# Inverse square roots moved from ten small VectorE steps to one GpSimd power operation

## The chip, the core and the metric

The kernel runs on one core of one Trainium2 chip. The metric is the device time of one execution in microseconds (us); three runs of the kernel before gave 2031.2, 2032.12 and 2036.46 us, median 2032.12 us. The engines are named as the profile names them: PE is TensorE (PEld its weight loads), DVE is VectorE, ACT is ScalarE, POOL is GpSimd, SP is SyncE, which here only issues DMAs.

## What is computed

One inference step of a two-layer decoder trunk of width 1024, for 1024 prompt tokens and 64 sample tokens with shared weights. Layer 0 is a gated short convolution beside a 4-head memory cross-attention, layer 1 is a multi-head latent attention of 8 heads beside another memory cross-attention; each has one input projection, a SiLU gate, one output projection and a residual. What matters here is how often an inverse root of a mean square occurs:

```python
def rms_norm(x, g):
    xf = x.astype(jnp.float32)
    y = xf * lax.rsqrt(jnp.mean(xf * xf, axis=-1, keepdims=True) + EPS)
    return (y * g.astype(jnp.float32)).astype(x.dtype)
```

It is taken of the tokens at the entry of both layers, of the memory and of its keys, of every memory query head (`mem_q_g`), of both latents of layer 1 (`q_lora_g`, `ckv_g`), of every query head, and, as `kscale = rsqrt(ms + EPS)`, of every key head of the latent attention.

## The kernel before

Activations lie feature-major, 128 features on the partitions and tokens along the free dimension, so a sum of squares over features is a matmul with ones. It gives a small tile of one value per token: 128 partitions by 1 to 16 columns. On this tile the inverse root is taken. A full-precision product is made of three matmuls (`mm3`, L189 to L191) on a value split into a high part (written by ACT, L183) and a low part, which is a subtraction of two SBUF tiles (`sub`, L179) on DVE or on POOL: the low parts of weights (`wli`, `wlo`, `wlv`) are mostly POOL's.

The prompt runs in two groups: A (256 prompt tokens and the 64 sample tokens) and B (768 prompt tokens). Two generators are interleaved: one does the memory keys and values, group B, the prompt attention of layer 1 (`mla`) and the last output product; the other does group A and the sample tokens, whose paged attention gathers its cache rows by indirect DMAs that POOL issues (`nat`, L1078). Within each engine the order of the instructions is then set by the scheduler of the tile framework, from its own estimates of durations; on the chip every engine works through its list in that order. So a change of one operation can move its neighbours.

The helper that the change rewrites and its callers, with the line numbers of the profile:

```python
196  def rsqrt_(p, out, v, shape):
202      V.tensor_scalar(out=out.bitcast(I32), in0=v.bitcast(I32), scalar1=-0.5, scalar2=float(0x5F3759DF), ...)
203      for _ in range(3):
204          V.tensor_tensor(out=t, in0=out, in1=out, op=ALU.mult)
205          V.scalar_tensor_tensor(out=t, in0=t, scalar=-0.5, in1=v, op0=ALU.mult, op1=ALU.mult)
206          V.scalar_tensor_tensor(out=out, in0=t, scalar=1.5, in1=out, op0=ALU.add, op1=ALU.mult)
...
478                  rsqrt_(pp, rs, v, [128, nt])
479                  V.tensor_scalar(out=rs, in0=rs, scalar1=MSC, scalar2=None, op0=ALU.mult)
...
1368         rsqrt_(p, rs, v, [128, 16])
1371         T.transpose(tk[0:8, 0:128], rs[:, 0:8], ident)
1379         V.scalar_tensor_tensor(out=rq, in0=rs[:, 8:16], scalar=SM, in1=rcq[:, 0:8], ...)
```

It is called 48 times: 16 times in `mem_part` (L478; tiles `mv_`, `mrs`; four heads, two layers, two groups), 9 times for the kv latent of layer 1 (L857; `cs1` to `cr1`, printed `cs` and `cr`, then `ckn` L859), 8 times in `prep` of the prompt attention (L1368; `akv` to `aks`, once per head, prepared while the head before is attended), and 15 times elsewhere (entry norms `strxa`, `strxb`, `strcq`, `strn`, memory `strm`, `ksr`, sample tokens `smr`, `ks_`, `rq`).

In the prompt attention each block of 128 queries is: scores on PE (L1410 to L1416), scaling by the key factor and running maximum on DVE (`ass`, L1418), the exponential on ACT (L1423), transposes of the weights on PE (`atp`, L1442) into one of two PSUM tiles, their split by ACT (`aPTH`) and DVE (`aPTL`, L179), and the value product on PE (`aO`).

Of the kernel before, what the change touches and what calls it, by code (L numbers as in the profile page):

```python
# [5 lines left out]
F = mybir.dt.float32  # L6
R = mybir.dt.float32r
I32 = mybir.dt.int32
# [16 lines left out]
EPS = 1e-6  # L25
# [59 lines left out]
# packed small vectors, one column each of [128, NV]  # L85
VG0, VG1, VGM, VGQL, VGQ, VGK, VMQ, VCW = 0, 8, 16, 32, 35, 36, 37, 39
NV = VCW + 24
# packed rows that are broadcast over partitions
# [4 lines left out]
def build(nc, tc, I, O):  # L93
# [50 lines left out]
    G.memset(ones, 1.0)  # L144
    rows = pc.tile([128, RMK], F, name="rows")
# [47 lines left out]
    cnt = [0]  # L193
    sm = {}

    def rsqrt_(p, out, v, shape):
        """out = v ** -0.5 by Newton steps from an integer seed."""
        cnt[0] += 1
        t = p.tile(shape, F, tag="rsq", name=f"rsq{cnt[0]}")
        P = shape[0]  # L200
        t, out, v = t[0:P], out, v
        V.tensor_scalar(out=out.bitcast(I32), in0=v.bitcast(I32), scalar1=-0.5, scalar2=float(0x5F3759DF), op0=ALU.mult, op1=ALU.add)
        for _ in range(3):
            V.tensor_tensor(out=t, in0=out, in1=out, op=ALU.mult)
            V.scalar_tensor_tensor(out=t, in0=t, scalar=-0.5, in1=v, op0=ALU.mult, op1=ALU.mult)
            V.scalar_tensor_tensor(out=out, in0=t, scalar=1.5, in1=out, op0=ALU.add, op1=ALU.mult)

    def stat_r(p, sqs, tiles, n, tag, eps=EPS, keep=None):
        """per token rsqrt(sum over features / n + EPS): [128, len(tiles)]; sqs: list of [128, T] squares."""
        nt = len(tiles)  # L210
        ps = pst("x", "stat" + tag)
        for i, (c0, m) in enumerate(tiles):
            for j, sq in enumerate(sqs):
                T.matmul(ps[0:m, 2 * i:2 * i + 2], sq[:, c0:c0 + m], ones[:, 0:2], start=(j == 0), stop=(j == len(sqs) - 1))
        v = (keep or p).tile([128, nt], F, name="stv" + tag, tag="stv" + (tag if keep else ""))
        r = (keep or p).tile([128, nt], F, name="str" + tag, tag="str" + (tag if keep else ""))
        if tiles[-1][1] < 128:
            V.memset(v, 1.0)
        for i0, i1, m in ([(0, nt, 128)] if tiles[-1][1] == 128 else [(0, nt - 1, 128), (nt - 1, nt, tiles[-1][1])]):
            V.tensor_scalar(out=v[0:m, i0:i1], in0=ps[0:m, 2 * i0:2 * i1].rearrange("p (i two) -> p i two", two=2)[:, :, 0], scalar1=1.0 / n, scalar2=eps, op0=ALU.mult, op1=ALU.add)  # L220
        rsqrt_(p, r, v, [128, nt])
        return v, r

    def bcast_tok(p, r, tiles, Tn, tag):
        """r [128 tokens, tile] -> list of (c0, n, psum [128, n]) with r along the free dim on all partitions."""
        out = []
        for b0 in range(0, len(tiles), 4):
            ts = tiles[b0:b0 + 4]
            ps = pst("s" if len(tiles) > 4 else "x", "bc" + tag)
            base_ = ts[0][0]  # L230
            for i, (c0, m) in enumerate(ts):
                d = p.tile([128, 128], F, name="dg" + tag, tag="dg", bufs=2)
                V.tensor_scalar(out=d[0:m, 0:m], in0=ident[0:m, 0:m], scalar1=r[0:m, b0 + i:b0 + i + 1], scalar2=None, op0=ALU.mult)
                T.matmul(ps[:, c0 - base_:c0 - base_ + m], ones[0:m, :], d[0:m, 0:m], start=True, stop=True)
            out.append((base_, ts[-1][0] + ts[-1][1] - base_, ps))
        return out
# [5 lines left out]
    def scale_T(xk, gcol, xH, xL):  # L242
        """split of x * g, not yet divided by the RMS"""
        for k in range(8):
            split_g(xH[:, k, :], xL[:, k, :], xk(k), gcol + k)

    def norm_T(pt, x, gcol, tiles, Tn, xH, xL, tag, le="g", ae=None, load=None):
        """x [128, 8, T] raw (feature-major) -> split of x * rsqrt(mean sq) * g."""
# [27 lines left out]
    class Stream:  # L276
        """weights: load two ahead, split one ahead."""
# [6 lines left out]
        def load_part(self, j, n):  # L284
            """one of n parts of the first unit"""
# [15 lines left out]
        def parts(self):  # L301
            """the splits of the next unit, as a list of calls"""
# [25 lines left out]
    def fm(ps, n, w, nk, xH, xL, c0):  # L328
        """feature-major product of one unit of 128 channels."""
# [96 lines left out]
    def mem_part(l, g, pp, ws, qi, xH, xL, ydst, done, pq, rb=None, fill=None):  # L426
        """memory attention of a group, head by head; ydst(h) holds the gate first and then the result"""
# [8 lines left out]
        def qpart(h, d):  # L436
            """q of head h: halves of q^T and the per token scale"""
# [100 lines left out]
    def samples(l, g, pp, nb):  # L538
        """memory attention of the sample tokens; the first step only starts loads"""
# [62 lines left out]
    def silu2(p, out, ps, n, rb=None):  # L602
        """out = 2 z sigmoid(z) = (tanh(z / 2) + 1) z, z = ps or ps * rb"""
# [7 lines left out]
    # persistent small tiles  # L611
# [109 lines left out]
    def out0(g, get, xsrc, acc, keep, px=None, held=None, wpre=()):  # L721
        """x1 = x + y W_out for the group; acc = sum of squares per feature row; held gets what remains to be done for the last unit"""
# [64 lines left out]
    def rope(p, out, src, cc, ss, m, nh, tag):  # L787
        """out, src [m, nh, 64]; cc, ss [m, 64]"""
# [9 lines left out]
    def in1_kv(g, ws, pp, xH, xL, rb):  # L798
        """latents: cq (feature-major), ckv and kpe (natural)"""
# [121 lines left out]
    def samp_prep():  # L921
# [23 lines left out]
        # k_nope of the own keys, only for their RMS factor  # L945
# [23 lines left out]
        # q  # L969
# [41 lines left out]
        # raw copies in (b, h, t) order  # L1011
# [13 lines left out]
        # scores against the own keys, all batches: [64 (h, t), b, 64 keys]  # L1025
# [25 lines left out]
    def samp_attn():  # L1051
        """keys 0..63 of a page on partitions 0..63 of the scores, keys 64..127 on the others, each with its own running maximum"""
# [4 lines left out]
        NU, UB, CU = 64, 8, 2  # units of 8 pages: all, in a batch row, in a softmax block  # L1057
# [157 lines left out]
    def mla_load(p):  # L1215
        """latents and tables that the preparation of the attention reads"""
        cq = p.tile([128, 3, NP], F, name="lcq")
        S.dma_start(out=cq, in_=d_cq)
        sm["pre"] = cq, rope_tab(p, 0, 8)
# [316 lines left out]
    def samp_y():  # L1536
        """sample attention output of layer 1: value up-projection and gate"""
# [28 lines left out]
    def out1_pre():  # L1566
        """first weights and gated branches of the output product, before the last head ends"""
# [68 lines left out]
    def group_a(g, xin):  # L1636
        """layer 0 for the first group of tokens; its result stays on chip, ready for layer 1"""
# [30 lines left out]
    def group_b(g, xin):  # L1668
        """layer 0 for the other tokens; gated branches and result wait in DRAM"""
# [63 lines left out]
    class Rows:  # L1733
        """separate tiles of features, read like one tile"""
# [45 lines left out]
    def interleave(a, b, rat):  # L1780
        """emit steps of a and b; in each part of b, a takes rat times the time of b; a waits at a name until b has passed it"""
# [157 lines left out]
```

## Time and profile before

| | before |
|---|---|
| time, median of three runs | 2032.12 us |
| span of the profiled execution, first to last instruction | 2030.3 us |
| mean granted TensorE clock over the span | 0.982 |
| PE busy | 1934.9 us, 95% |
| DVE busy | 979.2 us, 48% |
| ACT busy | 744.7 us, 37% |
| POOL busy | 669.5 us, 33% |
| DMA, mean | 181 GB/s |

The time of the profiled execution itself was not listed; its span is 1.8 us under the median and 0.9 us under the fastest run. An engine's share of busy time is an average over stages: PE is near full in most of them, and what is left of it idle lies in the first 50 us (32.0 us busy), between 150 and 200 us (37.5 us busy of 50), and in the prompt attention from 1570 to 1900 us (306.4 us busy of 330).

### The profile page before, as it was taken

What the parts mean: (1) busy time and instruction counts of PE and PEld (TensorE: products, weight loads), DVE (VectorE), ACT (ScalarE), POOL (GpSimd) and SP (SyncE); (2) the same over time, 40 slices, a digit from 0 to 9 for tenths busy, and PEclk for the clock granted to TensorE, in tenths of its full rate; (3) what the DMA queues carried; (4) which work ended last, traced back from release to release, by engine and by line L of the source; (5) the groups of instructions that cost most, each with busy time, mean ns of one, the idle gap of its engine ahead of it and who ended that gap; (6) DMA issues with size and microseconds to landing.
All of it is one profiled execution on the core that took longest, in us unless ns stands there. A gap on an engine that the chain in (4) does not pass through costs nothing. (4 is left out here: it accounts for less than half of the span.)

```text
span 2030.3 us, 33997 instructions
## 1 busy us (share of the span) xinstructions
PE 1934.9 (95%) x11740; PEld 1619.7 (80%) x11740; DVE 979.2 (48%) x2450; ACT 744.7 (37%) x1499; POOL 669.5 (33%) x589
## 2 busy tenths in 40 slices
PE   6997999999999999999999999999998899999999
PEld 5987998998997867667777765777687687787999
DVE  7659444456644533444323443344456656657300
ACT  6434323333321223333222322333333666667300
POOL 4544433422220223233434324333333334433220
PEclk8999999999999999999999999999999999999999
DMA  6552535442535487687988878877852311114532
GB/s 222 168 198 94 179 117 197 145 143 88 176 131 194 136 266 247 226 303 242 339 298 273 278 259 271 264 254 235 270 178 70 93 57 58 59 46 129 179 96 73
DMA packets 192877, 368.17 MB, mean 181 GB/s; under 512 B 27809, under 2 KB 135585, under 8 KB 191426
## 3 DMA queue, kind: packets, MB, share of 16 engines
q1 hardware_dynamic: 172178, 298.75, 44.7%
q0 software_dynamic: 20528, 67.26, 10.2%
q8 instruction: 93, 1.52, 0.3%
q14 instruction: 78, 0.64, 0.1%
HBM read 331.22 MB, written 34.70 MB: 180 GB/s over the span
## 5 line engine op out<-in xcount | busy, mean ns | idle before, releaser
L1078 POOL DMA_INDIRECT nat<-nat,IX x256 | 274.2, 1071 | 490.4 <-PE pv L1152 422.0
L189 PE MATMUL mm<-xH,whi 128*128 128x384 f32 (+1 forms) x1112 | 372.4, 335 | 9.7 <-ACT whi L183 5.1
L191 PE MATMUL mm<-xH,wli 128*128 128x384 f32 (+1 forms) x1112 | 367.1, 330 | 6.1 <-POOL wli L179 4.2
L190 PE MATMUL mm<-xL,whi 128*128 128x384 f32 (+1 forms) x1112 | 366.9, 330 | 0.8 <-DVE xL L179 0.8
L189 PEld LDWEIGHTS mm<-xH,whi 128*128 128x128 f32 x1112 | 213.8, 192 | 32.2 <-issue 13.3
L183 ACT ACTIVATE whi<-wri 128x1024 fp32r<-128x1024 f32 (+1 forms) x130 | 126.1, 977 | 271.1 <-PE mm L190 202.6
L191 PEld LDWEIGHTS mm<-xH,wli 128*128 128x128 f32 x1112 | 213.6, 192 | 8.3 <-POOL wli L179 5.3
L190 PEld LDWEIGHTS mm<-xL,whi 128*128 128x128 f32 x1112 | 213.8, 192 | 4.1 <-issue 2.4
L179 POOL TENSOR_TENSOR wli<-wri,whi 128x1024 fp32r<-128x1024 f32 (+1 forms) x65 | 146.9, 2264 | 161.2 <-ACT whi L183 161.0
L1087 PE MATMUL sAB<-rec,qar 128*64 128x512 f32 x512 | 153.5, 602 | 0.4 <-DMA rec<-rec 0.2
L1152 PE MATMUL pv<-nat,PT 128*64 128x256 f32 x1024 | 140.9, 392 | 4.8 <-ACT PT L1132 4.0
L1152 PEld LDWEIGHTS pv<-nat,PT 128*64 128x64 f32 x1024 | 75.6, 138 | 55.4 <-issue 13.5
L179 DVE TENSOR_TENSOR wli<-wri,whi 128x1024 fp32r<-128x1024 f32 (+1 forms) x65 | 72.8, 1124 | 72.1 <-ACT whi L183 69.9
L189 PE MATMUL mm<-nH,whi 128*128 128x384 f32 x304 | 105.6, 347 | 0.5 <-issue 0.5
L190 PE MATMUL mm<-nL,whi 128*128 128x384 f32 x304 | 102.4, 338 | 0.0
L191 PE MATMUL mm<-nH,wli 128*128 128x384 f32 x304 | 102.3, 337 | 0.0
L179 POOL TENSOR_TENSOR wlo<-wro,who 128x768 fp32r<-128x768 f32 (+3 forms) x30 | 59.2, 1978 | 118.0 <-ACT who L183 117.9
L189 PE MATMUL mm<-yHo,who 128*128 128x384 f32 (+1 forms) x288 | 97.1, 337 | 0.9 <-ACT yHo L183 0.9
L183 ACT ACTIVATE who<-wro 128x768 fp32r<-128x768 f32 (+3 forms) x44 | 38.1, 873 | 155.9 <-PE mm L190 117.7
L191 PE MATMUL mm<-yHo,wlo 128*128 128x384 f32 (+1 forms) x288 | 94.3, 327 | 0.0
L190 PE MATMUL mm<-yLo,who 128*128 128x384 f32 (+1 forms) x288 | 93.9, 326 | 0.0
L1089 PE MATMUL sAB<-rec,QPE 128*64 128x512 f32 x256 | 91.2, 596 | 0.0
(595 smaller groups left out, 4336.9 us busy)
## 6 DMA issues: line engine op xcount, KB each, us to landing
rec<-rec SPq DMA_DIRECT2D x512, 192.0 KB
wri<-wi SPq DMA_DIRECT2D x114, 512.0 KB
wro<-wo SPq DMA_DIRECT2D x29, 384.0 KB
smkv<-ckm SPq DMA_DIRECT2D x16, 512.0 KB
smkv<-cvm SPq DMA_DIRECT2D x16, 512.0 KB
wrm<-memw SPq DMA_DIRECT2D x7, 1024.0 KB
wro<-wo SPq DMA_DIRECT2D x7, 768.0 KB
yld<-d_ys SPq DMA_DIRECT2D x8, 544.0 KB
```

The lines of the kernel that those rows point to most:

```text
L179: eng.tensor_tensor(out=out, in0=a, in1=h.bitcast(F), op=ALU.subtract)
L183: A.activation(h, src, AF.Copy)
L189: T.matmul(out, wh, xh, start=first, stop=False)
L190: T.matmul(out, wh, xl, start=False, stop=False)
L191: T.matmul(out, wl, xh, start=False, stop=last)
L1078: G.indirect_dma_start(out=t[:, j % 2, :], out_offset=None, in_=I["nat"], in_offset=bass.IndirectOffsetOnAxis(ap=IX[:, q:q + 1], axis=0), ...
L1087: T.matmul(o, QA[:, cb, b, :], t[:, :, cb * 128 + ab * 64:cb * 128 + ab * 64 + 64], start=(cb == 0), stop=False)
L1089: T.matmul(o, QPE[:, b, ab, :], t[:, :, 256:320], start=False, stop=True)
L1152: T.matmul(d["v"][64 * ab:64 * ab + 64, 0:256], PT[:, j, ab, :], n[j][:, ab * 256:ab * 256 + 256], start=(i == 0 and j == 0), stop=(i == C ...
```

## The change

`rsqrt_` becomes one POOL instruction that raises the tile to the power -0.5, given as a constant tile `mhalf`, written once at the start. The scratch tile `rsq` goes away. Comments and docstrings are dropped too, so that line numbers after L144 are 2 higher, and after `rsqrt_` 7 lower.

```diff
     ones = pc.tile([128, 128], F, name="ones")
     G.memset(ones, 1.0)
+    mhalf = pc.tile([128, 16], F, name="mhalf")
+    G.memset(mhalf, -0.5)
...
     def rsqrt_(p, out, v, shape):
-        cnt[0] += 1
-        t = p.tile(shape, F, tag="rsq", name=f"rsq{cnt[0]}")
-        P = shape[0]
-        t, out, v = t[0:P], out, v
-        V.tensor_scalar(out=out.bitcast(I32), in0=v.bitcast(I32), scalar1=-0.5, scalar2=float(0x5F3759DF), op0=ALU.mult, op1=ALU.add)
-        for _ in range(3):
-            V.tensor_tensor(out=t, in0=out, in1=out, op=ALU.mult)
-            V.scalar_tensor_tensor(out=t, in0=t, scalar=-0.5, in1=v, op0=ALU.mult, op1=ALU.mult)
-            V.scalar_tensor_tensor(out=out, in0=t, scalar=1.5, in1=out, op0=ALU.add, op1=ALU.mult)
+
+        G.tensor_tensor(out=out, in0=v, in1=mhalf[0:shape[0], 0:shape[1]], op=ALU.pow)
```

The scheduler places the new instruction and what hangs on it anew. Three places show how. The first is DVE in the prompt attention, where the fourth head is prepared; before, the ten steps from `akv` to `aks`, of which the first seven are seen here, were mixed with the scaling of scores (`ass`) and the split of weights (`aPTL`):

```order
L1367 TENSOR_SCALAR akv<-akv 128x16
L202 TENSOR_SCALAR aks<-akv 128x16
L204 TENSOR_TENSOR rsq_21471<-aks 128x16
L205 SCALAR_TENSOR_TENSOR rsq_21471<-rsq_21471,akv 128x16
L206 SCALAR_TENSOR_TENSOR aks<-rsq_21471,aks 128x16
L204 TENSOR_TENSOR rsq_21471<-aks 128x16
L205 SCALAR_TENSOR_TENSOR rsq_21471<-rsq_21471,akv 128x16
L1418 ISA ass,amx<-mm,akb 128x512
L1418 ISA amx 128x1
L206 SCALAR_TENSOR_TENSOR aks<-rsq_21471,aks 128x16
L179 TENSOR_TENSOR aPTL<-atp,aPTH 128x4x128
```

The same stretch of DVE in the changed kernel:

```order
L1360 TENSOR_SCALAR akv<-akv 128x16
L1372 SCALAR_TENSOR_TENSOR arq<-aks,rcq 128x8
L1411 ISA ass,amx<-mm,akb 128x512
L1411 ISA amx 128x1
L181 TENSOR_TENSOR aPTL<-atp,aPTH 128x4x128
```

The reader of the result, `arq`, has moved up from behind all ten steps to the place directly behind their input, ahead of `ass` and `aPTL`. On POOL, in the same stretch, the splits of values (`avH`, `avL`) and of weights (`wlv`) stood alone before:

```order
L1310 CAST avH<-araw 128x512
L179 TENSOR_TENSOR avL<-araw,avH 128x512
L1310 CAST avH<-araw 128x512
L179 TENSOR_TENSOR avL<-araw,avH 128x512
L179 TENSOR_TENSOR wlv<-wrv,whv 128x512
```

and now have the power among them:

```order
L1303 CAST avH<-araw 128x512
L181 TENSOR_TENSOR avL<-araw,avH 128x512
L1303 CAST avH<-araw 128x512
L199 TENSOR_TENSOR aks<-akv,mhalf 128x16
L181 TENSOR_TENSOR avL<-araw,avH 128x512
L181 TENSOR_TENSOR wlv<-wrv,whv 128x512
```

It stands behind the second cast and ahead of that cast's subtraction. The second place is PE in that stretch, where `tk` is the transpose that reads the result:

```order
L1416 MATMUL mm<-cmb,idb 128x128
L1442 MATMUL atp<-ident,ass 128x128 x4
L189 MATMUL aO<-aPTH,avH 128x256
L1410 MATMUL mm<-akH,aqH 128x512
L1442 MATMUL atp<-ident,ass 128x128
L190 MATMUL aO<-aPTL,avH 128x256
```

In the changed kernel the rows at this point are:

```order
L1409 MATMUL mm<-cmb,idb 128x128
L1364 MATMUL tk<-ident,aks 8x128
L1435 MATMUL atp<-ident,ass 128x128 x5
L191 MATMUL aO<-aPTH,avH 128x256
L192 MATMUL aO<-aPTL,avH 128x256
```

`tk`, which stood six rows below the first piece, is now ahead of the transposes `atp`, and one value product and one score product that stood between the fourth and the fifth `atp` now come behind the fifth. The third place is DVE in the memory attention of layer 0, group A, third head, where `yr` is the gate and `xL` a low part for group B:

```order
L477 TENSOR_SCALAR mv__1978<-mst 128x2
L202 TENSOR_SCALAR mrs<-mv__1978 128x2
L204 TENSOR_TENSOR rsq_1981<-mrs 128x2
L205 SCALAR_TENSOR_TENSOR rsq_1981<-rsq_1981,mv__1978 128x2
L179 TENSOR_TENSOR xL<-xnxb,xH 128x768
L609 SCALAR_TENSOR_TENSOR yr_442<-slt,mm 128x320
```

In the changed kernel:

```order
L470 TENSOR_SCALAR mv__1910<-mst 128x2
L181 TENSOR_TENSOR xL<-xnxb,xH 128x768
L602 SCALAR_TENSOR_TENSOR yr_424<-slt,mm 128x320
L472 TENSOR_SCALAR mrs<-mrs 128x2
L265 SCALAR_TENSOR_TENSOR xnxb<-x,vec,bcxb 128x256
```

Three of the ten steps stood ahead of `xL` and `yr`; now nothing does, and the scaling of the result (L472) comes behind both.

## Rows read from the trace of the kernel before

**Rows 1.** The page: the span, the busy time of each engine with its share of the span and its instructions, and the TensorE clock that was granted, in tenths of full speed, in 40 equal slices of the span.

```profile
span 2030.3 us, 33997 instructions
PE 1934.9 (95%) x11740; PEld 1619.7 (80%) x11740; DVE 979.2 (48%) x2450; ACT 744.7 (37%) x1499; POOL 669.5 (33%) x589
...
PEclk8999999999999999999999999999999999999999
```

**Rows 2.** Busy time by window, of the instructions that read or write the scratch tile `rsq` alone (L204 to L206, nine of the ten steps of each call), over the whole span; then the clock and the DMA share of that stretch.

```profile
0.00:2030.30 2030.30, 98.32 (x432) 0.98 0.55 181
```

**Rows 3.** The waits of PE: who waited <- for whom: us in total, times, longest us.

```profile
PE atp L1442 <- DVE rsq L204: 7.0, 5, 2.4
...
PE mst L471 <- DVE msq L452: 4.1, 2, 3.7
PE mm L189 <- DVE yr L609: 4.1, 2, 3.6
...
PE ckt L873 <- DVE ckn L859: 3.3, 3, 2.4
```

**Rows 4.** The timeline in the prompt attention where the fourth head is prepared: start us, length us, engine, line, operation, out<-in, shape, count, and in brackets the idle time before it and what ended it. DVE first, then POOL, then PE.

```profile
1685.17 0.18 DVE L1367 TENSOR_SCALAR akv<-akv 128x16 f32<-128x16 f32 x1
...
1686.30 1.16 DVE L206 SCALAR_TENSOR_TENSOR aks<-rsq,aks 128x16 f32<-128x16 f32 x1
...
1689.51 0.68 DVE L179 TENSOR_TENSOR aPTL<-atp,aPTH 128x512 fp32r<-128x512 f32 x1
...
1685.41 0.62 POOL L1310 CAST avH<-araw 128x512 fp32r<-128x512 f32 x1 [2.77 <-ACT araw L1309]
1686.11 1.31 POOL L179 TENSOR_TENSOR avL<-araw,avH 128x512 fp32r<-128x512 f32 x1
1687.38 1.27 POOL L179 TENSOR_TENSOR wlv<-wrv,whv 128x512 fp32r<-128x512 f32 x1
...
1690.34 0.30 PE L1442 MATMUL atp<-ident,ass 128*128 128x128 f32 x1 [2.38 <-DVE rsq L204]
```

**Rows 5.** The same timeline where the third head is prepared and POOL has nothing to do; DVE, then PE.

```profile
1646.41 0.17 DVE L1367 TENSOR_SCALAR akv<-akv 128x16 f32<-128x16 f32 x1
...
1648.45 0.68 DVE L179 TENSOR_TENSOR aPTL<-atp,aPTH 128x512 fp32r<-128x512 f32 x1
...
1647.95 0.39 PE L189 MATMUL aO<-aPTH,avH 128*128 128x256 f32 x1 [0.24 <-ACT aPTH L183]
1648.18 0.40 PE L1410 MATMUL mm<-akH,aqH 128*128 128x512 f32 x1
1649.28 0.30 PE L1442 MATMUL atp<-ident,ass 128*128 128x128 f32 x1 [0.70 <-DVE rsq L204]
```

**Rows 6.** The same timeline where the first head is prepared: DVE's first step, and PE's transpose of the result.

```profile
1583.61 0.17 DVE L202 TENSOR_SCALAR aks<-akv 128x16 int32<-128x16 int32 x1
...
1589.09 0.27 PE L1371 MATMUL tk<-ident,aks 128*8 128x128 f32 x1 [2.60 <-DVE aks L206]
```

**Rows 7.** The timeline of layer 0, group A, memory attention, third head: DVE, POOL, PE.

```profile
176.23 1.74 DVE L204 TENSOR_TENSOR rsq<-mrs 128x2 f32<-128x2 f32 x1
178.00 2.27 DVE L205 SCALAR_TENSOR_TENSOR rsq<-rsq,mv__1978 128x2 f32<-128x2 f32 x1
...
181.06 0.47 DVE L609 SCALAR_TENSOR_TENSOR yr<-slt,mm 128x320 f32<-128x320 f32 x1
...
173.78 2.38 POOL L179 TENSOR_TENSOR wli<-wri,whi 128x1024 fp32r<-128x1024 f32 x1 [7.46 <-ACT whi L183]
176.13 1.82 POOL L179 TENSOR_TENSOR xL<-xnxb,xH 128x768 fp32r<-128x768 f32 x1
177.92 2.33 POOL L179 TENSOR_TENSOR wli<-wri,whi 128x1024 fp32r<-128x1024 f32 x1
...
181.59 0.64 PE L189 MATMUL mm<-xH,whi 128*128 128x320 f32 x1 [3.62 <-DVE yr L609]
```

**Rows 8.** Two windows by engine: start and end, length, then busy us (instructions) of PE, PEld, DVE, ACT and POOL, the granted clock, the DMA share and GB/s.

```profile
179.60:186.40 6.80, 4.81 (x19) 4.81 (x20) 6.34 (x18) 1.47 (x2) 1.08 (x2) 0.50 0.24 77
1589.30:1592.70 3.40, 3.40 (x13) 2.82 (x12) 0.50 (x3) 0.41 (x1) 0.00 (x0) 0.50 0.44 130
```

**Rows 9.** POOL's groups by line and shape: the two small operations with two input tiles; busy us, mean ns of one, then the idle time before.

```profile
L794 POOL TENSOR_TENSOR rp2k<-kg,rtab 128x64 f32<-128x64 f32 x8 | 2.6, 328 | 39.2 <-DVE kg L862 33.1 <-DMA rec<-rec 5.9
...
L161 POOL TENSOR_TENSOR gq<-vec 128x1 f32<-128x1 f32 x1 | 0.2, 190 | 1.4 <-DMA vec<-vec 1.4
```

**Rows 10.** The timeline near the start, at the entry norm of group A: POOL, then PE.

```profile
24.47 4.66 POOL L179 TENSOR_TENSOR wlm<-wrm,whm 128x1024 fp32r<-128x1024 f32 x2 [3.65 <-ACT whm L183]
...
31.18 1.81 PE L234 MATMUL bcxa<-dgxa,ones 128*128 128x128 f32 x6 [5.97 <-DVE dgxa L233]
```

**Rows 11.** The timeline at one of the nine calls for the kv latent, while POOL issues gathers: DVE's first step and the reader of the result, then POOL.

```profile
1251.44 0.15 DVE L202 TENSOR_SCALAR cr<-cs 128x1 int32<-128x1 int32 x1
...
1253.56 0.48 DVE L859 SCALAR_TENSOR_TENSOR ckn<-mm,cr,rows 128x256 f32<-128x256 f32 x1 [0.21 <-DVE cr L206]
...
1251.37 1.01 POOL L1078 DMA_INDIRECT nat<-nat,IX  x1 [0.30 <-issue]
```

**Rows 12.** The timeline of DVE in the memory attention of layer 1, group A, first head: the first of the ten steps, and the reader of the result.

```profile
476.70 2.23 DVE L202 TENSOR_SCALAR mrs<-mv__4885 128x2 int32<-128x2 int32 x1
...
481.79 0.16 DVE L494 SCALAR_TENSOR_TENSOR mnb<-mmx,mrs 128x2 f32<-128x2 f32 x1
```

More of the change, by code (lines that the diff above doesn't have):

```diff
@@ L191, in mm3 @@
         T.matmul(out, wl, xh, start=False, stop=last)
-    cnt = [0]
     sm = {}
     def rsqrt_(p, out, v, shape):
-        cnt[0] += 1
-        t = p.tile(shape, F, tag="rsq", name=f"rsq{cnt[0]}")
-        P = shape[0]
-        t, out, v = t[0:P], out, v
-        V.tensor_scalar(out=out.bitcast(I32), in0=v.bitcast(I32), scalar1=-0.5, scalar2=float(0x5F3759DF), op0=ALU.mult, op1=ALU.add)
-        for _ in range(3):
-            V.tensor_tensor(out=t, in0=out, in1=out, op=ALU.mult)
-            V.scalar_tensor_tensor(out=t, in0=t, scalar=-0.5, in1=v, op0=ALU.mult, op1=ALU.mult)
-            V.scalar_tensor_tensor(out=out, in0=t, scalar=1.5, in1=out, op0=ALU.add, op1=ALU.mult)
+        G.tensor_tensor(out=out, in0=v, in1=mhalf[0:shape[0], 0:shape[1]], op=ALU.pow)
     def stat_r(p, sqs, tiles, n, tag, eps=EPS, keep=None):
```

## The prediction

> **What bounds the kernel now.** I read the page first: PE is busy for 95% of the span of 2030.3 us and the other engines for 48% or less [rows 1]. So only what PE waits for, or what lowers its clock, can move the time. The ten DVE steps are not small in total: the nine steps that touch the scratch tile are 432 instructions and 98 us of DVE time [rows 2], more than their usual 0.16 to 0.18 us each, and the seeds come on top. But nearly all of it lies beside PE's work. So the second view is the list of PE's waits [rows 3], to see where DVE's steps reach PE. Four entries can be theirs: the transposes `atp` of the prompt attention (7.0 us), a product of layer 0 that waits for a gate `yr` (4.1 us), the sums `mst` that wait for `msq` (4.1 us), and the transposes `ckt` that wait for `ckn` (3.3 us). The third view is the timeline at these places.
>
> It shows why some calls take long. Where POOL is idle, the ten steps take what they are worth [rows 5]. Where POOL runs an operation on SBUF tiles, a DVE step on SBUF tiles stretches until POOL's operation is over: 1.16 us in place of 0.17, ending with POOL's `avL` [rows 4], and 1.74 and then 2.27 us, ending with POOL's `xL` and `wli` [rows 7]. DVE's own splits `aPTL`, which read PSUM, are not stretched. So each call is a row of chances to be held, and what stands behind it on DVE, and PE behind that, is held too.
>
> **What the change does, part by part.** It removes ten DVE steps per call and adds one POOL operation, a trip DVE to POOL to DVE, and a place in POOL's list.
>
> *The price of the power.* No row before shows one. From below it is not less than the smallest two-tile operation on POOL, 0.19 us; the nearest in kind is `rp2k`, 0.33 us [rows 9]. From above I take ten POOL passes of the latter, 3.3 us, as if POOL did what DVE did step by step. I take 0.8 us, the geometric middle, above the nearest row because a power is more than a product. The trip adds about 0.1 us each way.
>
> The Trainium skill ("GPSIMD Engine Reference", section "Engine selection") speaks against the change: elementwise work with two inputs belongs on VectorE, GpSimd being about twice as slow. By that figure the power would be about 0.33 us, twice a DVE step, and the sum below would come to some 2013 us instead; what the rule leaves out is that ten steps become one.
>
> *Layer 0, group A, third head.* DVE's steps 2 and 3 were held by POOL's `xL` and `wli` and ended at 180.2; `yr` came at 181.06 and PE waited 3.62 us for it [rows 7]. In the new order `xL` and `yr` stand ahead of anything that needs the power. `yr` can come when `xL` is done, some 3.5 us earlier; this wait goes: -3.6 us. Behind it the granted clock was 0.50, the lower level (1.2 in place of 2.4 GHz), for 6.8 us [rows 8], worth 3.4 us; without the wait I take it as gone: -3.4 us.
>
> *Layer 1, group A, first head.* The reader `mnb` came at 481.79, after a first step held for 2.23 us [rows 12]. With a power at 476.7 to 477.5 its scaling can still be held once by the POOL operation that follows (2.4 us, like the `wli` in rows 7), so it comes near 480.1: 1.7 us earlier, in a chain that ends in the 3.7 us wait for `msq` [rows 3]: -1.7 us.
>
> *The kv latent, nine calls.* Ten steps take from 1251.44 to 1253.3, then `ckn` [rows 11]. In the new list the power stands behind the gather that started at 1251.37, so it starts at 1252.4 and gives `ckn` near 1253.3: 0.3 us earlier. This is the call with the longest queue ahead; at a free POOL it is 0.9 us earlier. Of the 3.3 us that PE waits [rows 3] I take 1: -1.0 us. Gathers queued behind a power should not be short of time: in the whole list of PE's waits none names a gather.
>
> *Prompt attention, first head.* The steps start at 1583.61 and PE waits 2.60 us for their result, until 1589.09 [rows 6]; the clock then stays at 0.50 for 3.4 us [rows 8], worth 1.7 us. In the new order the power is ahead of POOL's other work there and PE has value products around `tk`: -4.3 us.
>
> *Heads with POOL idle (second, third, fifth, seventh).* Their input is ready at 1646.6; before, `aPTL` starts at 1648.45 [rows 5]. Now DVE stands still at `arq` for about 1.0 us, then does `arq`, `ass` (0.68) and `aPTL`: again near 1648.4. But one value and one score product, 0.6 us of PE work from 1647.95 to 1648.58, which filled this wait, now come behind the fifth `atp`. Each such head loses 0.6 us: +2.4 us.
>
> *Heads with POOL busy (fourth, sixth, eighth).* Input at 1685.35, cast until 1686.0, power until 1686.8; then `avL` runs and holds `arq` (two SBUF tiles) until 1688.1, and `aPTL` follows near 1689.0, 0.5 us earlier than 1689.51 [rows 4]. The same 0.6 us of PE work has moved behind: 0.
>
> *The start.* PE waits 5.97 us for the entry norm, which is held behind two POOL subtractions of 4.66 us together [rows 10]. The power now stands ahead of both; but its reader, a one-tile operation on SBUF, then meets them, as the seeds met POOL in rows 12. I count 0 (up to -4 if the reader gets through first).
>
> *Sum:* -3.6 - 3.4 - 1.7 - 1.0 - 4.3 + 2.4 = -11.6 us. All other calls lie beside full PE work; if that cover were gone, they would save or lose the difference between 1.0 and some 1.9 us each. Against the span of 2030.3 that is 2018.7; the span is 1.8 us under the median of the runs, so 2020.5; I say **2020 us**.
>
> **The rivals.**
> *Slower: the power is long.* DVE stands at `arq` with `ass` and `aPTL` behind it, in seven heads, and PE waits for `ckn` in nine calls: 16 us for each microsecond of price. The sum is zero at 1.5 us, and 0.3% slower from about 1.9 us. At 3.3 us it is 2060. For it: a power is no single product, and 16 columns may cost far more than one. Against it: every small POOL row. Chance 18%.
> *No change: the holding moves.* DVE's other two-tile steps (`xL`, `anb`, `arq`) and the scalings take over the stretches that the Newton steps suffered, because POOL's long subtractions stay as they are. Then layer 0 gives 2 of its 7 us, the clock stays down, and the prompt attention gains only the first head's 2.6: about -4 us, 2028. For it: POOL's operations are not fewer, and each reader comes just when POOL goes on. Against: `yr` no longer has a Newton step ahead. The Trainium skill ("GPSIMD Engine Reference", "Key points") says that GpSimd shares its SBUF interfaces with VectorE, in contention with instructions in a 2-port mode or with two SBUF inputs; by that rule each reader of a power is exposed, and the trace agrees (1.16 us in rows 4). Chance 22%.
> *More gain: a cheap power.* At 0.3 us or less the 16 waits give another 8 us, and if the clock in the later heads stays up and the start gives 4, it ends near 2003. Chance 7%.
>
> **How the numbers follow.** The forecast (0.3 to 1.2 us, stretches gone as listed) has 53%, with its own range 2011 to 2026. The range for 8 in 10 goes from 2005 to 2040: it leaves out the better half of the cheap power and the power above some 2.2 us. A difference of under 0.3% (6 us) can't be told from no change. Faster than that: forecast and cheap power, 60%; within: 22%; slower: 18%.
>
> **What would show it.** DVE's busy time falls by about 110 us and POOL's rises by 48 powers, some 20 to 40 us. PE's wait for `yr` (3.62 us) and for the first `tk` (2.60 us) are gone, with the lower clock behind them. The wait of the fifth `atp` is longer, not shorter, in the heads where POOL is idle, and DVE's idle time is named by the power ahead of `arq`. I am wrong if the power takes more than 1.5 us, if PE waits at `tk`, or if gathers behind a power come late for the paged attention.

## The result: 0.6% slower

The changed kernel took 2041.74 us, median of seven runs (2038.41 to 2045.17); the kernel before, on the same chip, took 2029.54 us (2024.72 to 2036.46). The ratio is 1.006, 95% interval 1.0043 to 1.0078: about 12 us slower, where 2020 us had been forecast. It also lies just outside the range, which ended at 2040. Everything below is told as ratios to runs of the kernel before on the same chip in the same hour, since its median moved between 2022 and 2030 us from one set of runs to another.

The page of the profiled execution (2038.41 us, of which the span is 2036.6), to be read beside [rows 1]:

```profile
span 2036.6 us, 33564 instructions
...
PE 1933.1 (95%) x11740; PEld 1626.6 (80%) x11740; DVE 902.4 (44%) x1970; ACT 745.8 (37%) x1499; POOL 729.8 (36%) x638
...
PEclk8998999989999999999999999999999998999999
```

DVE is 77 us less busy and POOL 60 us more. PE's busy time is the same, and so is its share; the longer span is idle time of PE. Its waits name the place. Before, the transpose `tk` and the transposes `atp` behind `aPTL` stood at this:

```profile
PE atp L1442 <- DVE aPTL L179: 8.5, 10, 2.2
...
PE tk L1371 <- DVE aks L206: 3.4, 2, 2.6
```

Now these two entries are the largest, and the `rsq` entry of [rows 3] is gone:

```profile
PE tk L1364 <- POOL aks L199: 17.2, 8, 2.8
PE atp L1435 <- DVE aPTL L181: 15.3, 14, 1.9
...
PE mtr L505 <- DVE mv__2049 L470: 3.3, 1, 3.3
...
PE mtr L505 <- DVE mv__1910 L470: 2.4, 1, 2.4
```

`tk` is the transpose that reads the 16-column root of a head in the prompt attention. It waits for the power eight times, 2.15 us each on average. The groups of the power by shape, from the line of the helper (name, count, then minimum, median and maximum in ns, first and last start, shape), say why:

```profile
L199 POOL TENSOR_TENSOR cr<-cs,mhalf x9: 530/559/590, 438.1 to 1252.6; 128x1 f32<-128x1 f32 x8, 64x1 f32<-64x1 f32 x1
L199 POOL TENSOR_TENSOR aks<-akv,mhalf x8: 2898/2900/2930, 1573.3 to 1842.7; 128x16 f32<-128x16 f32 x8
L199 POOL TENSOR_TENSOR smr<-smv,mhalf x4: 547/550/1467, 297.7 to 606.4; 128x1 f32<-128x1 f32 x4
L199 POOL TENSOR_TENSOR ksr<-ksv,mhalf x2: 1634/1634/1635, 49.8 to 100.8; 128x8 f32<-128x8 f32 x2
...
L199 POOL TENSOR_TENSOR strxa<-stvxa,mhalf x1: 890/890/890, 27.4 to 27.4; 128x3 f32<-128x3 f32 x1
L199 POOL TENSOR_TENSOR strm<-stvm,mhalf x1: 695/695/695, 48.0 to 48.0; 128x2 f32<-128x2 f32 x1
```

A power of one column takes 0.56 us, of two 0.70, of eight 1.63 and of sixteen 2.90. From 1 to 16 columns that is (2.90 - 0.56) / 15 = 0.156 us for each further column, and the widths between lie near this line. The forecast had one price, 0.8 us, for every width.

The timeline of the third head (its counterpart before is in [rows 5]): DVE's last step before the power, POOL, PE, and DVE again.

```profile
1636.12 0.18 DVE L1360 TENSOR_SCALAR akv<-akv 128x16 f32<-128x16 f32 x1
...
1636.38 2.90 POOL L199 TENSOR_TENSOR aks<-akv,mhalf 128x16 f32<-128x16 f32 x1 [4.93 <-DVE akv L1360]
...
1639.33 0.27 PE L1364 MATMUL tk<-ident,aks 128*8 128x128 f32 x1 [2.38 <-POOL aks L199]
1639.44 0.69 PE L1435 MATMUL atp<-ident,ass 128*128 128x128 f32 x4
...
1640.90 0.45 PE L1435 MATMUL atp<-ident,ass 128*128 128x128 f32 x1 [0.77 <-DVE aPTL L181]
...
1639.31 0.17 DVE L1372 SCALAR_TENSOR_TENSOR arq<-aks,rcq 128x8 f32<-128x8 f32 x1 [3.01 <-POOL aks L199]
...
1640.07 0.69 DVE L181 TENSOR_TENSOR aPTL<-atp,aPTH 128x512 fp32r<-128x512 f32 x1
```

Two readers stand at the power at once. PE stands at `tk` for 2.38 us; DVE stands at `arq` for 3.01 us, so `aPTL` behind it ends at 1640.76 and the fifth `atp`, which needs the PSUM tile that `aPTL` reads, waits another 0.77 us. What follows is in two windows (length, busy us of PE, PEld, DVE, ACT, POOL, granted clock, DMA share, GB/s), and behind them the whole prompt attention:

```profile
1639.30:1642.80 3.50, 2.70 (x14) 2.40 (x15) 2.23 (x9) 2.16 (x3) 0.00 (x0) 0.57 0.01 2
1643.00:1646.40 3.40, 3.40 (x12) 2.82 (x11) 1.71 (x5) 1.70 (x3) 0.00 (x0) 0.50 0.32 92
1570.00:1900.00 330.00, 292.52 (x1859) 248.73 (x1860) 172.43 (x520) 206.74 (x397) 136.56 (x123) 0.96 0.25 78
```

The same 330 us of the kernel before:

```profile
1570.00:1900.00 330.00, 306.37 (x1949) 258.80 (x1950) 199.72 (x610) 216.37 (x413) 118.08 (x118) 0.98 0.27 85
```

For some 7 us behind the first wait PE runs at or near its lower level (0.50, 1.2 GHz); but for the second wait it is fully occupied there. So this head pays 2.38 + 0.77 us of waiting, where the old one paid 0.70 [rows 5], and 2 to 3 us of clock: about 5 us together.

How far the profiled kernels differ inside the prompt attention can be read in the timeline without what went before: from the last of the four transposes of `ast` (the step ahead of the root) of the first head to that of the eighth. Before it is 1582.1 to 1837.6, that is 255.5 us; now 1571.7 to 1841.2, that is 269.5 us. The changed kernel enters 10 us earlier and has lost that lead by the sixth head.

### The profile page after: what moved, and what is told of

Read it like the earlier page. It is cut to its first block, busy times and chain, and to the rows that moved or that the text cites. A ratio compares the mean times of both kernels' runs of the same rounds, so it can differ in the third digit from the quotient of the medians.

```text
span 2036.6 us, 33564 instructions
## 1 busy us (share of the span) xinstructions
PE 1933.1 (95%) x11740; PEld 1626.6 (80%) x11740; DVE 902.4 (44%) x1970; ACT 745.8 (37%) x1499; POOL 729.8 (36%) x638
## 5 line engine op out<-in xcount | busy, mean ns | idle before, releaser
L181 DVE TENSOR_TENSOR wli<-wri,whi 128x1024 fp32r<-128x1024 f32 (+1 forms) x65 | 76.9, 1189 | 78.9 <-ACT whi L185 77.3
```

Source lines behind the costliest of these rows:

```text
L181: eng.tensor_tensor(out=out, in0=a, in1=h.bitcast(F), op=ALU.subtract)
```

## Experiments

The theory after the result, called A: the loss is the price of the eight 16-column powers, and everything else is a gain. The rivals: the loss comes from the new order of `tk` and the transposes (O), or is POOL's or the program's in general (B), or the lead that the changed kernel had is slack (C).

### Undo the prompt attention alone, and do it alone

```
-            rsqrt_(p, rs, v, [128, 16])
+            newton_(p, rs, v, [128, 16])      # the ten VectorE steps of before
```

> The changed kernel with one call undone: the eight 16-column roots of the prompt attention (the call in prep) go back to the ten VectorE steps, the other 40 stay powers. The order of the instructions before the prompt attention is that of the changed kernel, inside it that of the kernel before. Theory A (the price by columns: the changed kernel was 10 us ahead where the prompt attention began and lost 17 us in it, since a 16-column power takes 2.90 us): the 10 us stay and the 17 go, about 2020 us where the kernel before has 2030, a ratio of 0.995. Rival B (the loss is not this operation's, but belongs to a chain that is only seen in the prompt attention, for instance POOL's splits being later everywhere): within 4 us of the changed kernel, 2038 to 2042. Rival C (the 10 us ahead are slack that is spent at the start of the prompt attention anyway): 2028 to 2032.

Measured: 0.9969 (0.9953 to 0.9984), 6.3 us faster than the kernel before. The converse has `newton_` in all calls but this one:

> The converse: powers in the eight calls of the prompt attention alone, the ten VectorE steps in the other 40. Theory A: the loss without the gain, 15 to 18 us over the kernel before, about 2046 us, a ratio of 1.008. Rival B: no slower than the kernel before, 2028 to 2034. Rival C: as the changed kernel, 2040 to 2044, since what comes ahead of the prompt attention makes no difference.

Measured: 1.0085 (1.0057 to 1.0113), 17 us slower. From `ast` of the first head to the eighth the two took 255.1 and 272.2 us. Theories B and C of the expectations fall: +17 and -6 are 11, beside the 12 measured for the whole change. The gain outside is smaller than the 10 us that the two profiles had suggested. The reason is in the profiles: the converse runs the old steps ahead of the prompt attention, like the kernel before, and still entered it 6.6 us ahead of that kernel's profiled execution; between 900 and 1277 us alone it gained 7.9 us on it, with the same steps in both. So much of the 10 us was variation between executions.

### The order kept, the price taken away; the order kept, the price doubled

```
-            rsqrt_(p, rs, v, [128, 16])
+            G.tensor_tensor(out=rs, in0=v, in1=mhalf, op=ALU.subtract)
```

This kernel leaves out the root of the eight heads.

> The changed kernel with a subtraction in place of the power in the eight calls of the prompt attention, on the same tiles, so the query and key factors of those heads are wrong values. Every engine's list is otherwise that of the changed kernel. It keeps the order and takes away the price. Theory A: the operation takes 0.2 to 0.4 us, PE's waits for tk (17.2 us in all) shrink to below 3 us and the stretches of lower clock behind them go: 2018 to 2024 us. Rival O (the order costs: tk and one product have changed places with the transposes, whatever the power takes): most of the loss stays, 2034 to 2040 us.

Measured: 0.9923 (0.9896 to 0.9949), 15.6 us faster than before, 28 us faster than the changed kernel, with the same lists on all engines in the prompt attention. The subtraction takes 0.22 us:

```profile
L1361 POOL TENSOR_TENSOR aks<-akv,mhalf x8: 220/220/223, 1573.6 to 1818.6; 128x16 f32<-128x16 f32 x8
```

PE's wait at `tk` was 0.13 us in the first head and nil in the others, and the stretch of seven heads took 245.1 us. The gain is larger than A said, which had put it at 2018 to 2024 us against 2030 (0.994 to 0.997), though the interval reaches that range.

```
+            rs0 = p.tile([128, 16], F, name="aks0", tag="aks0")
+            rsqrt_(p, rs0, v, [128, 16])
             rsqrt_(p, rs, v, [128, 16])
```

> The changed kernel with the power of the prompt attention issued twice in each of the eight heads (the first result is not used), the order otherwise the same. Theory A: nothing hides the price at tk, so the eight waits grow by 2.9 us each, 23 us, and by some us more of lower clock: 2063 to 2075 us. Rival O: the wait at tk is set by something else or is partly covered, less than 12 us more, 2042 to 2053 us.

Measured: 1.0213 (1.0182 to 1.0243), 43 us slower than before. In the second head DVE now takes `aPTL` ahead of `arq`; all else in the prompt attention stands as in the changed kernel. The eight waits at `tk` went from 17.2 to 40.2 us, by the 23 that A said:

```profile
PE tk L1366 <- POOL aks L199: 40.2, 8, 5.7
```

With the changed kernel the three lie on a line within their intervals: at 0.22, 2.90 and 5.80 us of price the time stands at -15.6, +12.2 and +43.1 us to the kernel before. That is 27.8 / 2.68 = 10.4 us for each microsecond of price in the first step and 30.9 / 2.90 = 10.7 in the second, each known to some 2 us. The change breaks even at about 0.22 + 15.6 / 10.4 = 1.7 us. O falls: with the same order a cheap operation is worth 16 us.

### Which of the two readers pays

> The changed kernel, but from the second head on the transpose tk and the copies behind it are written one block of queries later. On PE tk then stands a block behind the transposes atp; on DVE arq, the other reader of the power, stays where it was, ahead of ass and aPTL; POOL's list is that of the changed kernel. Theory D (two readers: DVE is held at arq as long as PE was at tk, and aPTL behind it frees the PSUM tile for the fifth atp near 1640.8 in the third head in any case): the wait goes from tk to atp, and the time stays within 6 us of the changed kernel, a ratio to the kernel before of 1.003 to 1.007. Theory T (PE's wait at tk is the whole loss): as with a cheap operation, 0.990 to 0.996.

```
             rsqrt_(p, rs, v, [128, 16])
             yield 1.0
+            if h:
+                yield 1.0
```

Measured: 1.0061 (1.0041 to 1.008), no better than the changed kernel. In the third head PE passes the transposes now, and then waits 2.85 us at the fifth, until 1640.66, near the 1640.8 of the expectation:

```profile
1640.66 0.45 PE L1437 MATMUL atp<-ident,ass 128*128 128x128 f32 x1 [2.85 <-DVE aPTL L181]
```

The other reader alone, `arq` as two POOL operations behind the power (0.20 and 0.27 us), `tk` in its place:

```
+            G.tensor_tensor(out=rq, in0=rs[:, 8:16], in1=rcq[:, 0:8], op=ALU.mult)
+            G.tensor_scalar(out=rq, in0=rq, scalar1=SM, scalar2=None, op0=ALU.mult)
...
-            V.scalar_tensor_tensor(out=rq, in0=rs[:, 8:16], scalar=SM, in1=rcq[:, 0:8], op0=ALU.mult, op1=ALU.mult)
```

> The changed kernel with arq computed by POOL, in two small operations behind the power, and nothing else: on DVE no reader of the power stands ahead of ass and aPTL any more, on PE tk stands where it was. With the two runs before it makes a square: neither reader moved (the changed kernel, 1.006), tk alone (1.0061), both (0.9956). Theory D (either reader alone is enough to hold the head for the price): no real gain, 1.003 to 1.007. Theory T2 (DVE's wait at arq is the whole loss): 0.994 to 0.998.

Measured: 1.0015 (1.0001 to 1.0029). Neither expectation: less than half of the loss is left, though PE still waits 17.4 us at `tk`. The timeline of its third head and the two windows behind the wait:

```profile
1635.61 0.27 PE L1367 MATMUL tk<-ident,aks 128*8 128x128 f32 x1 [2.41 <-POOL aks L199]
```

```profile
1635.50:1639.00 3.50, 3.39 (x24) 3.18 (x25) 1.33 (x5) 2.35 (x5) 0.52 (x3) 1.00 0.01 2
1639.00:1642.40 3.40, 3.40 (x23) 2.85 (x23) 3.13 (x8) 2.34 (x5) 1.47 (x2) 1.00 0.69 237
```

The wait at `tk` is as long as in the changed kernel, but the 0.77 us at the fifth `atp` is gone, and the clock is 1.00 where the changed kernel had 0.57 and 0.50. From the third to the fourth head it takes 41.1 us in place of 44.8, so in this head more is gained than the length of the second wait. That the second wait brought the lower clock isn't shown: in the fifth head of the same run the same wait stands alone, and the lower level follows all the same.

```profile
1714.91 0.27 PE L1367 MATMUL tk<-ident,aks 128*8 128x128 f32 x1 [2.41 <-POOL aks L199]
```

```profile
1715.70:1719.10 3.40, 3.40 (x16) 3.21 (x15) 0.75 (x3) 2.01 (x5) 0.00 (x0) 0.50 0.01 2
1570.00:1900.00 330.00, 299.19 (x1929) 257.77 (x1930) 174.68 (x512) 209.93 (x399) 145.96 (x141) 0.98 0.26 83
```

That head takes 42.6 us in place of 43.7. Over the whole prompt attention the clock was 0.98 in place of 0.96, PE's waits for `aPTL` fell from 15.3 to 9.2 us, and the seven heads took 260.3 us in place of 269.5, which is the 9 us between the two ratios. Both readers moved:

> As the run with tk a block later, and arq is computed by POOL too, by two small operations right behind the power, so that neither PE nor DVE has a reader of the power near it. The powers stay everywhere, at 2.90 us each in the prompt attention. Theory D: now nothing waits for the power; the gain of the cheap operation comes back, a ratio of 0.989 to 0.995, 12 to 22 us under the kernel before. Rival Q (POOL itself is the limit: avL, wlv, aqp come 3.5 us later and PE or ACT waits for them, or the key factors akb come late for the next head since their DMA starts a block later): 0.999 to 1.006.

Measured: 0.9956 (0.9941 to 0.9972), 9 us faster than before, with the 2.90 us powers all in place; the interval reaches the range of theory D and stays clear of Q's. Of the seven waits at `tk` from the second head on none is left. The square is 1.006 (neither), 1.0061 (`tk`), 1.0015 (`arq`), 0.9956 (both): each reader alone can hold the head. Left alone, DVE's keeps the whole loss and PE's less than half of it. Rival Q is there in small: the next head once came late since its key factors are loaded from what `tk` gives (the second row is DVE's, which ends the first row's wait).

```profile
1693.87 0.98 PE L1438 MATMUL atp<-ident,ass 128*128 128x128 f32 x5 [2.92 <-DVE anb L1417]
...
1692.82 0.29 DVE L1414 CUSTOM_DVE_ANT_0 ass<-mm,akb 128x128 f32<-128x128 f32 x1 [3.57 <-DMA akb<-d_ks]
```

So `tk` was moved less far, behind the products of its own block, `arq` again on POOL:

```
-                next(nxt, None)
+                if i != 6:
+                    next(nxt, None)
                 if len(pend) > MLAG:
                     step(*pend.pop(0))
                 if SLAG == 1:
                     scale(i, ss, ls)
+                if i == 6:
+                    next(nxt, None)
```

> arq by POOL as before, and tk moved less far: from the second head on it stands behind the transposes and value products of its own block, some 4 us of PE work behind the input of the power and half a block ahead of the run with tk a block later. There the next head once waited 2.9 us since the key factors akb, which are loaded from what tk gives, landed late. Theory D: neither the power nor the load is waited for, 0.990 to 0.995, better than 0.9956. Rival: PE waits at tk again since 4 us are too short for the input, the power and the trip, 0.996 to 1.002.

Measured: 0.9954 (0.9938 to 0.997). PE no longer waits at `tk` from the second head on, so the rival's wait is not there, but the gain over the run before can't be told from nothing: from the second head to the eighth DVE still waits for `akb` four times, 8.2 us in all, and PE once 3.0 us behind it.

### Where the gain outside the prompt attention sits

Three kernels put the old steps back in more places than the first of these experiments: also in the kv latent, also in the memory attention, and in both.

```
-            rsqrt_(pp, r1[0:m], s1[0:m], [m, 1])
+            newton_(pp, r1[0:m], s1[0:m], [m, 1])
```

> The ten VectorE steps in the eight calls of the prompt attention and in the nine of the kv latent; the other 31 calls stay powers. The run with VectorE steps in the prompt attention alone was at 0.9969. In the changed kernel the lead grew from 2.7 us at 715 us to 13 us at 1277 us and was 10 us at 1500 us, and all nine calls of the kv latent but the first lie in that stretch or just ahead of it. Theory K (the kv latent is worth 6 to 9 us, not the 1 us of the forecast): most of the gain goes, 0.999 to 1.002. Rival (it is worth the 1 us): 0.996 to 0.998.

Measured: 0.9966 (0.9948 to 0.9984): the rival's range, and theory K falls.

```
-                    rsqrt_(pp, rs, v, [128, nt])
+                    newton_(pp, rs, v, [128, nt])
```

> The ten VectorE steps in the eight calls of the prompt attention and in the sixteen of the memory attention; the other 24 calls stay powers. Theory M (the memory attention gives its 5 us at the first head of layer 1, where the lead went from -1 to 5 us between 453 and 620 us, and loses nothing): 0.999 to 1.001. Rival (what the memory attention gains there it loses at the start of layer 0, where the changed kernel was 3 us behind): 0.996 to 0.998.

Measured: 0.9978 (0.9962 to 0.9994): in the rival's range, with an interval that just reaches theory M's, so the two aren't told apart.

> Powers only in the 15 calls outside the prompt attention, the kv latent and the memory attention: entry norms, memory and its keys, sample tokens; VectorE steps in the other 33. With VectorE steps in the prompt attention alone the ratio was 0.9969, with the kv latent added 0.9966, with the memory attention added 0.9978. Theory N (the gain sits in the 15 calls): 0.996 to 0.998. Rival (it sits in the sum of the kv latent and the memory attention, each too small to tell by itself): 0.999 to 1.001.

Measured: 1.0026 (1.0016 to 1.0037), slower than before, outside both expectations. By times alone: powers in the 15 other calls cost 5 us; adding the kv latent's or the memory attention's gives 10 to 12 us back, and adding both (0.9969) gives no more than one. The timeline shows a place that behaves so: the first head of the memory attention in layer 1, where the sums `mst` wait for `msq` [rows 3]. The row of that wait in the kernel before, in the kernel with powers in the 15 others alone, in that with the kv latent's added, in that with the memory attention's added, and in the changed kernel with both:

```profile
490.74 0.98 PE L471 MATMUL mst<-ones,msq 128*128 128x2 f32 x4 [3.66 <-DVE msq L452]
```

```profile
494.45 0.58 PE L473 MATMUL mst<-ones,msq 128*128 128x2 f32 x4 [3.66 <-DVE msq L454]
```

```profile
492.84 0.58 PE L473 MATMUL mst<-ones,msq 128*128 128x2 f32 x4 [2.13 <-DVE msq L454]
```

```profile
487.01 0.58 PE L473 MATMUL mst<-ones,msq 128*128 128x2 f32 x4 [0.63 <-DVE msq L454]
```

```profile
488.51 0.50 PE L464 MATMUL mst<-ones,msq 128*128 128x2 f32 x4
```

Against the kernel before the five gain 0, 0.7, 5.5, 6.5 and 8.0 us between the transposes of the kv latent at 462 us and the sums `sst` of the sample tokens at 589 us. All the profiled kernels with powers in both places gained 8.0 to 8.1 us there, and the one with old steps in all of it (the converse) 0.9. So this chain is shown, and that either call shortens most of it. What makes powers in the 15 others slower by 0.3% isn't shown in full. Two places show in the timelines of PE, set against the kernel before. Between 25 and 60 us, at the entry norm of group A, the eleven profiled kernels with powers there lost 0.8 to 1.7 us, the two with old steps there 0.1 at most. Between 660 and 690 us, at the query heads of the sample tokens, the eleven lost 0.7 to 3.5 us and the two nothing; there PE waits for `qr`, whose chain starts with a power of eight columns, and in none of the three kernels with old steps there does it wait for it:

```profile
669.93 0.64 PE L1002 MATMUL qpT<-ident,qr 64*64 64x64 f32 x8 [1.14 <-DVE qr L789]
```

In the kernel with powers in the 15 others alone the two come to 1.9 of its 5 us. The kernel that keeps the old steps there and has all else of the run with `tk` behind its own block's products was run last.

> The run with arq on POOL and tk behind its own block's products (0.9954), with the 15 calls outside the prompt attention, the kv latent and the memory attention put back to the ten VectorE steps. Theory N2 (those 15 calls cost 0.3% of their own, as they did alone at 1.0026, by a start that is some 3 us later): 0.991 to 0.994. Rival (that 0.3% belongs to how the calls fall together, not to those 15): 0.9945 to 0.997.

Measured: 0.994 (0.9922 to 0.9959), 12 us faster than before; the best of the kernels that compute the root, but its interval overlaps with that of 0.9954, so by times the 15 calls stay open.

## Why the prediction was wrong

**The step that failed is the price of the power.** The forecast took 0.8 us "above the nearest row because a power is more than a product", for all 48 calls. For one and two columns that was close (0.56 and 0.70 us). For 16 columns it was wrong by 3.6 times, and these eight calls are the ones that PE waits for. The nearest row pointed the wrong way: `rp2k`, a product of 64 columns in 0.33 us [rows 9], says that columns cost almost nothing, and for a product or the subtraction above (0.22 us) that holds. The power costs by the column. The upper bound, ten POOL passes at 3.3 us, came near by chance. A range of prices by width was to be had: the forecast's own rival said that "16 columns may cost far more than one", and then gave it 18% and a constant price.

The Trainium skill ("GPSIMD Engine Reference", section "Engine selection") puts two-input elementwise work on GpSimd at about twice VectorE's time. The trace agrees for wide subtractions (`wli` of 128x1024 takes 2.45 us on POOL and 1.26 on DVE in the changed kernel). At 16 columns the subtraction is nearer to DVE's time (0.22 us beside 0.18 for a Newton product of that shape), and the power of the same tile is 13 times the subtraction, so the rule can't price a power.

**The rate was right in kind, too low for a head.** The rival "the power is long" put 1 us on each microsecond of price in seven heads and in nine calls of the kv latent, 16 us in all, with the break-even at 1.5 us. The runs changed the price of the 16 columns alone: eight heads, 10.4 to 10.7 us, so that each pays 1.3 us for a microsecond, and by interpolation 1.7 us as the break-even. The nine calls were not varied; with powers of 0.56 us PE's waits for `ckn` fell from 3.3 to 0.7 us. On the measured line a price of 0.8 us would have given -15.6 + 0.58 x 10.4, about -10 us, beside the -11.6 of the sum. That is interpolated, not run, and the nearness is luck in part, since outside the prompt attention one term came out ten times too large and another nearly five times too small (below).

**The heads.** "DVE stands still at `arq` for about 1.0 us", with `ass` and `aPTL` behind it, was the right mechanism, with 3.01 us in place of 1.0. What was missed is PE: in the new order `tk` stands ahead of the transposes, so PE waits too, and in five of the eight heads the lower clock follows (in four before, for less time). The forecast booked +0.6 and 0 us for a head. By the timeline the step from the third to the fourth head, prepared with POOL idle, went from 39.9 to 44.8 us; the next, prepared with POOL busy, from 36.9 to 38.9. The first head was to give 4.3 us since PE had value products around `tk`; PE waits 2.85 us there in place of 2.60 [rows 6].

**Layer 0, third head, -7.0 us: wrong, and here the rival "the holding moves" came true.** The wait for `yr` is gone, as forecast. In its place:

```profile
178.69 1.85 POOL L181 TENSOR_TENSOR xL<-xnxb,xH 128x768 fp32r<-128x768 f32 x1
181.48 1.34 POOL L199 TENSOR_TENSOR mrs<-mv__1910,mhalf 128x2 f32<-128x2 f32 x1 [0.93 <-DVE mv__1910 L470]
182.79 2.36 POOL L181 TENSOR_TENSOR wli<-wri,whi 128x1024 fp32r<-128x1024 f32 x1
...
180.58 0.75 DVE L265 SCALAR_TENSOR_TENSOR xnxb<-x,vec,bcxb 128x512 f32<-128x512 f32 x1 [1.33 <-POOL xL L181]
181.24 0.15 DVE L470 TENSOR_SCALAR mv__1910<-mst 128x2 f32<-128x2 f32 x1
181.31 0.95 DVE L181 TENSOR_TENSOR xL<-xnxb,xH 128x768 fp32r<-128x768 f32 x1
182.18 0.48 DVE L602 SCALAR_TENSOR_TENSOR yr<-slt,mm 128x320 f32<-128x320 f32 x1
182.85 2.32 DVE L472 TENSOR_SCALAR mrs<-mrs 128x2 f32<-128x2 f32 x1 [0.19 <-POOL mrs L199]
...
181.45 0.65 PE L505 MATMUL mtr<-ident,mP 128*128 128x128 f32 x4 [2.35 <-DVE mv__1910 L470]
```

DVE waits for POOL's `xL` to free a buffer, `mv_` behind it is late, and PE waits 2.35 us at `mtr`, which writes into the one PSUM tile of its kind, from which `mv_` has to read first. The scaling `mrs` is held for 2.32 us by the `wli` that starts beside it. The clock from 186 to 196 us was 0.84. The lag of the changed kernel behind the one before was 3.3 us at 147 us and 2.6 us at 294 us: 0.7 us gained, not 7.

**Layer 1, first head, -1.7 us: right place, too small.** It gave 8.0 us. The forecast saw one call 1.7 us earlier "in a chain that ends in the 3.7 us wait for `msq`" and took only the call's own lead. The wait went whole, and the lower clock behind it too.

**The kv latent, -1.0 us:** not told from zero beside the powers of the memory attention (0.9966 with the old steps in it, 0.9969 without). **The start, 0:** at 60 us the changed kernel was 3.3 us behind, but the converse, with the old steps there, was 3.1 us behind too, and both had most of it at 25 us, ahead of the first root. What the powers cost there is the 0.8 to 1.7 us told above.

Inside the prompt attention the sum said -1.9 and the runs say +17; outside it said -9.7 and the runs say -6.3. DVE's busy time fell by 77 us, not 110, and POOL's rose by 60, not 20 to 40: the powers' own time. Some of what DVE has left took longer, the 16 scalings `mrs` 13.6 us in place of 4.1, so the holding moved in more places than in the third head of layer 0.

## What to carry to other kernels

A price for an operation that the trace has never shown should be asked for by width, not once: which calls are wide, and does PE stand behind just those? Count both readers of a result, on each engine's list, since moving PE's alone gave nothing here (1.0061), moving DVE's alone under half of what both gave (1.0015), and moving both gave back most of the price (0.9956, beside 0.9923 with the cheap operation). A long operation on an engine with time to spare costs little once nobody in order has to wait for it: the same eight powers of 2.90 us stand in the kernel at 1.006 and in those at 0.9954 and 0.994.

## What the runs showed of the hardware

The power does not hold DVE as POOL's subtractions do [rows 4, 7]. In the run with both readers moved, DVE's small steps on SBUF tiles keep their usual time while a power runs, the one with two input tiles (`anb`) in all seven heads in which it falls there:

```profile
1636.39 2.93 POOL L199 TENSOR_TENSOR aks<-akv,mhalf 128x16 f32<-128x16 f32 x1 [4.93 <-DVE akv L1360]
...
1637.18 0.16 DVE L1420 RECIPROCAL als<-als 128x1 f32<-128x1 f32 x1 [0.87 <-ACT ass L1419]
...
1639.11 0.16 DVE L1417 SCALAR_TENSOR_TENSOR anb<-amx,arq 128x1 f32<-128x1 f32 x1
```

The power itself can be held: in the rows of layer 0 above, two columns took 1.34 us in place of 0.70 beside DVE's `xL`, which kept its 0.95 us. The Trainium skill ("GPSIMD Engine Reference", section "Key points") tells of contention with DVE instructions that run in a 2-port mode or have two SBUF inputs. `xL` has two, and the trace agrees, with POOL as the side that was delayed; `anb` has two SBUF inputs as well, and beside the power the trace shows no contention (0.16 us), so there the measurement differs from the page; in the changed kernel `anb` took up to 1.27 us, beside POOL's subtractions. The other powers that were held also ran beside such subtractions of DVE: one column took 1.47 us in place of 0.55 beside `wli`, and six columns 1.81 in place of 1.35 beside `mkL`. The scaling `mrs`, held for 2.32 us, has one SBUF tile as its input; whether DVE ran it in a 2-port mode no trace shows.

What brings the lower clock isn't settled by these runs. Where DVE's reader alone was moved, a single wait of 2.41 us for `tk` left the granted clock at 1.00 in the third head and was followed by 0.50 in the fifth. Behind the 2.85 us of the first head it stayed at 1.00 in the changed kernel and fell to 0.50 in that run:

```profile
1576.40:1583.00 6.60, 6.51 (x39) 4.99 (x38) 1.58 (x4) 2.67 (x5) 4.33 (x4) 1.00 0.37 98
```

```profile
1572.40:1575.60 3.20, 3.20 (x16) 3.20 (x17) 0.88 (x2) 0.24 (x1) 2.94 (x4) 0.50 0.01 3
```
